# The last product pair of each output tile: 512 columns first, 256 columns second

## The chip, the cores and the metric

The kernel runs on one core of a Trainium2 chip. The metric is device time in microseconds, from runs that are timed without a profile; the kernel before has a median of 1256.36 us over 3 runs (1256.25 to 1256.43). Beside them there is one profiled execution with its trace.

## The reference

One layer of a streaming encoder over 256 positions and 2048 channels, in float32:

```python
h = _rmsnorm(x, norm_mix[i])
proj = h @ w_in[i]                                  # 2048 -> SSD and GLA inputs
mix = jnp.concatenate([y_ssd, y_gla], axis=-1) @ w_out[i]
x = x + mix
h = _rmsnorm(x, norm_ffn[i])
u = _causal_dwconv(h @ ffn_w_up[i], ffn_conv_w[i], ffn_conv_b[i])   # 2048 -> 11264
gate, val = jnp.split(u, [D_FF], axis=-1)
x = x + (jax.nn.silu(gate) * val) @ ffn_w_down[i]   # 5632 -> 2048
pg = jax.nn.sigmoid(_rmsnorm(x, norm_ple[i]) @ ple_w_gate[i])       # 2048 -> 2048
x = x + pg * (p[i] @ ple_w_proj[i])
return _rmsnorm(x, norm_final)
```

The change concerns the products from `w_out` on. The two mixers in front of them (a Mamba-2 scan and a gated linear attention) are left as they are.

## The kernel before

Everything is held with channels on the 128 partitions and the 256 positions along the free dimension. Weights stream from DRAM in chunks of 1 MB: a chunk (`raw`) holds 16 blocks of 128 x 128. ACT rounds each half chunk to float32r (`whi`, L185), and DVE takes the remainder (`wlo`, L186); the pool has 5 buffers of each, so two to three chunks are ready ahead of TensorE. Activations are split in the same way, into `act[:, 0, :]` (rounded) and `act[:, 1, :]` (remainder).

A block (m, k) of a weight contributes to output tile m in a PSUM bank of 512 columns. In the helper `mm2` one product has the rounded weights against both parts of the activation side by side, 512 columns wide (the hi product, L219); a second has the remainder of the weights against the rounded activation, 256 columns wide, into the lower half of the bank (the lo product, L220). For the last block of an output tile (`last`) the two stand the other way round: lo at L220, then hi at L222 with the stop flag. `mm3`, with three products of 256 columns, serves the input projection and the very last tile of the gate.

`project` walks a sequence of (m, k): the blocks of the first two tiles are interleaved, so that their last 4 or 5 k come after both; from the third tile on, a tile's blocks follow one another. A chunk is 16 blocks; with 16 blocks to a tile (output projection, up-projections, gate) a tile from the third on is one chunk, with 22 (down-projections) chunks begin in the middle of tiles. `project` is called six times: output projection (16 tiles of 16 blocks), up-projection (44 of 16) and down-projection (16 of 22) for the first half of the hidden width, the same for the second half, and the gate (16 of 16, the last through `mm3`).

When a tile's last product is issued, `evac` takes it: after the output and the down-projections DVE adds both halves of the bank to x (L917); after the up-projections and the gate ACT copies the upper half (L232) and DVE adds the lower (L233). Output tiles rotate over four banks (`pm_t`). TensorE's order is the program's order, written out by hand; ACT's, DVE's and the DMA queue's rows are ordered by a scheduler that works with dependences and an estimated timeline, in which the weight chunks have a raised priority. At the start of the first up-projection and of the gate, norms of the residual stream run between the products (`norm_task`), and the evictions that need the norm's result (`rb`, L331) follow it.

Of the kernel before, what the change touches and what calls it, by code (L numbers as in the profile page):

```python
# [15 lines left out]
T = 256  # L16
# [65 lines left out]


def steps(n_m, n_k, tail):
    """(m, k) in the order of the products: the last k of the first two m come after both."""
    cut = n_k - tail
    s = [(m, k) for m in (0, 1) for k in range(cut)]
    s += [(m, k) for m in (0, 1) for k in range(cut, n_k)]
    return s + [(m, k) for m in range(2, n_m) for k in range(n_k)]


SEQ16 = steps(16, KT, 4)
SEQ_UP = steps(2 * UPH, KT, 4)
SEQ_DN = steps(16, UPH, 5)


@with_exitstack
def trunk(ctx, tc, wst, wv, xin, pin, prm_d, cst_d, gku_d, out):
    nc = tc.nc
    V, S, G, PE = nc.vector, nc.scalar, nc.gpsimd, nc.tensor  # L100
# [12 lines left out]
    def slot(dtype=F32, shape=(128, 512)):  # L113
        return gpool.tile(list(shape), dtype, name="slot")
# [4 lines left out]
    def pmt():  # L119
        return pm.tile([128, 512], F32, name="pm_t")  # L120

    def pxt():
        return px.tile([128, 512], F32, name="px_t")
# [1 line left out]
    def v3(ap, n):  # L125
        return ap.rearrange("p (a b) -> p a b", a=n)

# [1 line left out]
    now = [0]  # L129
    tasks = []  # L130
    done = {}
# [1 line left out]
    def tick():  # L133
        now[0] += 1
        for t in list(tasks):
            if t[0] <= now[0]:
                d = next(t[1], None)
                if d == 0:
                    continue
                if d is None:  # L140
                    tasks.remove(t)
                else:
                    t[0] = now[0] + d
                break
# [8 lines left out]
        while any(done.get(k, 1 << 30) > now[0] for k in keys):  # L153
            yield 0

# [1 line left out]
    ready = {}  # L157

    def raw_tile():
# [45 lines left out]
    def chunk(c):  # L205
        load(c)
        load(c + 1)
        return ready.pop(c)

    def lhs(wt, j):  # L210
        hi, lo = wt[j // 8]
        w = slice((j % 8) * 128, (j % 8 + 1) * 128)
        return hi[:, w], lo[:, w]

    def mm2(ps, wt, j, act, first, last):
        hi, lo = lhs(wt, j)
        both = act.rearrange("p a t -> p (a t)")
        if not last:
            PE.matmul(ps, lhsT=hi, rhs=both, start=first, stop=False)  # L219
        PE.matmul(ps[:, 0:T], lhsT=lo, rhs=act[:, 0, :], start=False, stop=False)  # L220
        if last:
            PE.matmul(ps, lhsT=hi, rhs=both, start=False, stop=True)  # L222

    def mm3(ps, wt, j, act, first, last):
        hi, lo = lhs(wt, j)
        PE.matmul(ps, lhsT=hi, rhs=act[:, 0, :], start=first, stop=False)  # L226
        PE.matmul(ps, lhsT=hi, rhs=act[:, 1, :], start=False, stop=False)  # L227
        PE.matmul(ps, lhsT=lo, rhs=act[:, 0, :], start=False, stop=last)  # L228
# [5 lines left out]
        return t  # L234

    def project(base, seq, acts, n_k, evac, single=None):
        """Products of a weight stream in the order seq; evac(m, ps) when an output tile is whole."""
        ps = {}
        wt = None
        for n, (m, k) in enumerate(seq):  # L240
            if n % 16 == 0:
                wt = chunk(base + n // 16)
            if k == 0:
                ps[m] = pmt()
            if m == single:
                mm3(ps[m][:, 0:T], wt, n % 16, acts[k], k == 0, k == n_k - 1)
            else:
                mm2(ps[m], wt, n % 16, acts[k], k == 0, k == n_k - 1)
            if k == n_k - 1:
                evac(m, ps.pop(m))  # L250
            if n % TICK == TICK - 1:
                tick()

# [1 line left out]
    def pcol(i):  # L255
        return prm[:, i:i + 1]

# [73 lines left out]
        S.copy(out=keep, in_=ps)  # L331
        then(r, keep)

# [1 line left out]
    prm = const.tile([128, NPRM], F32, name="prm")  # L335
    x = const.tile([128, KT, T], F32, name="x")
    cst = const.tile([128, NCST], F32, name="cst")
# [33 lines left out]
    for m in range(KT):  # L371
        wt = ready[m // 8]
        if m % 2 == 0:
            ps = pmt() if m % 4 == 0 else pxt()
# [19 lines left out]
    for a in proj:  # L394
        store_proj(*a)

# [1 line left out]
    usuf_r = const.tile([128, 128], F32R, name="usuf_r")  # L398
    ones_r = const.tile([128, 128], F32R, name="ones_r")
    cbh = const.tile([128, 12], F32, name="cbh")  # L400
# [38 lines left out]
        S.activation(out=t, in_=c, func=AF.Tanh)  # L439
        V.scalar_tensor_tensor(out=out, in0=t, scalar=1.0, in1=c, op0=ALU.add, op1=ALU.mult)  # L440

# [1 line left out]
    gkl = const.tile([32, T], F32, name="gkl")  # L443
    G.memset(gkl, 1.0)
    dta = const.tile([128, 32], F32, name="dta")
# [73 lines left out]
        PE.matmul(ps[:, 16:32], lhsT=tri, rhs=a_tm[:, 16:32], start=True, stop=True)  # L519
        S.activation(out=esuf, in_=ps[:, 0:32], func=AF.Exp)  # L520

# [1 line left out]
    ssd_x = [None] * 8  # L523
    bT = slot()
    cT = slot()
# [194 lines left out]
                    mix[i] = split(y)  # L720
            yield from norm_task(ssd_sq[g], 512, then, 9)

# [1 line left out]
    gq = [slot(), slot()]  # L724
    gk = [slot(), slot()]
    gla = {}
# [119 lines left out]
        V.tensor_tensor(out=o, in0=o, in1=sg, op=ALU.mult)  # L846
        mix[8 + i] = split(o)

# [1 line left out]
    def ev_in(kind, i, ps):  # L850
        if kind == "conv":
            ev_conv(i, ps)
        elif kind == "q":
            ev_qk(gq, i, ps, 128.0 ** -0.5)
        elif kind == "k":
            ev_qk(gk, i, ps, 1.0)
            mark(("k", i))
        elif kind == "z":
            ev_z(i, ps)
        else:  # L860
            ev_g(i, ps)

    vps = None
    for ci, (kind, i) in enumerate(PLAN):
# [20 lines left out]
        if kind == "v":  # L885
# [3 lines left out]
            for kk in range(4):  # L889
                k = kc * 4 + kk  # L890
                hi, lo = wt[kk // 2]
# [11 lines left out]
        else:  # L903
            ps = pmt()
# [6 lines left out]
    while tasks:  # L911
        tick()

# [1 line left out]
    def add_res(i, ps):  # L915
        for h in range(2):
            V.tensor_tensor(out=x[:, i, :], in0=x[:, i, :], in1=ps[:, h * T:(h + 1) * T], op=ALU.add)  # L917
# [8 lines left out]
    sq_ffn = SumSq()  # L926
    xf = [None] * KT
    project(OFF_OUT, SEQ16, mix, KT, residual(sq_ffn, P_GFFN, xf))

# [1 line left out]
    state.clear()  # L931

    def delayed(f):
# [42 lines left out]
    for half in range(2):  # L976
        base = OFF_F0 if half == 0 else OFF_F1
        project(base, SEQ_UP, xf, KT, ev_up(half))
        if half == 0:
            project(base + N_UP, SEQ_DN, hid, UPH, add_res)  # L980
        else:
            sq_ple = SumSq()
            project(base + N_UP, SEQ_DN, hid, UPH, residual(sq_ple, P_GPLE, xg))

# [1 line left out]
    state.clear()  # L986
    sq_fin = SumSq()
    emb = {}
# [52 lines left out]
    start(first_emb())  # L1041
    project(OFF_GATE, SEQ16, xg, KT, delayed(ev_gate), single=KT - 1)

# [1 line left out]
    banks = {}  # L1045

    def turn(q, c):
# [126 lines left out]
```

## Time and profile before

| what | value |
|---|---|
| median of the timed runs | 1256.36 us (1256.25 to 1256.43) |
| profiled execution, first to last instruction (its span) | 1254.4 us |
| median less span | 1.96 us |
| TensorE products, busy | 1243.2 us (99%), 7707 products |
| TensorE weight loads, busy | 1110.7 us (89%) |
| DVE, ACT busy | 896.0 us (71%), 691.2 us (55%) |
| DMA share, mean HBM rate | 52.4%, 183 GB/s |
| mean granted TensorE clock | 0.999 |

The profiled execution has no time of its own other than its span; what lies around the span is taken as the difference to the median. Products overlap in the records: a 512-column product's row is some 398 ns long, yet the next one starts 0.24 us after it. What a product costs in a stream is therefore read from start to start and not from its length. The stages start at 313.25 (output projection), 403.68 (first up-projection), 652.88 (first down-projection), 777.23 (second up-projection), 1025.97 (second down-projection) and 1150.32 us (gate); the last tile's three-product blocks start at 1235.57.

### The profile page before, as it was taken

Reading aid. Unit: us, or ns where it says so; the run is one execution under the profiler, and the core shown is the slowest. Engines: PE = TensorE matmul, PEld = TensorE weight load, DVE = VectorE, ACT = ScalarE, POOL = GpSimd, SP = SyncE. Lnnn points to the kernel's source line nnn. Section 1 sums busy time; section 2 is a strip of 40 time slices with the busy share of each in tenths; the row PEclk is TensorE's granted clock in tenths of the full one; section 3 lists DMA queues with packets and bytes.
Section 4 is the critical chain, followed back from the end, with each engine's and each line's share of the span. In section 5 each row is a group of like instructions: output and inputs, shape, how many; then the busy total and the mean of one; then the engine's idle time right before and its main releaser. Section 6 shows DMA issues by size and latency. Waiting matters only on the chain.

```text
span 1254.4 us, 19554 instructions
## 1 busy us (share of the span) xinstructions
PE 1243.2 (99%) x7707; PEld 1110.7 (89%) x7707; DVE 896.0 (71%) x1531; ACT 691.2 (55%) x1144; POOL 2.9 (0%) x10
## 2 busy tenths in 40 slices
PE   9999999999999999999999999999999999999997
PEld 7999999999888888888888888888888888888886
DVE  7877665788777787777775555777777776666775
ACT  8685564565545565555553333555555554444664
POOL 0000000000000000000000000000000000000000
PEclk9999999999999999999999999999999999999999
DMA  9745353344555455555555555555555555556531
GB/s 332 295 156 172 124 202 135 137 167 168 198 174 199 168 202 173 196 179 191 187 183 193 178 197 174 198 173 197 183 186 191 179 196 193 199 172 223 197 131 67
DMA packets 36830, 231.01 MB, mean 184 GB/s; under 512 B 4209, under 2 KB 4593, under 8 KB 11138
## 3 DMA queue, kind: packets, MB, share of 16 engines
q1 hardware_dynamic: 36738, 229.76, 52.4%
q8 instruction: 60, 0.98, 0.3%
q14 instruction: 32, 0.26, 0.1%
HBM read 225.55 MB, written 4.19 MB: 183 GB/s over the span
## 4 chain that ended last, share of the span: by engine, by line
PE 97%; DVE 1%; ACT 1%; DMA 1%; SPq 0%; issue 0%; DVEq 0%
PE pm_t L219 46%; PE pm_t L220 25%; PE pm_t L226 6%; PE pm_t L228 6%; PE pm_t L227 6%; PE pm_t L222 3%; PE pm_t L897 1%; PE pm_t L898 1%; PE pm_t L896 1%; DMA raw<-in_wst_dram 1%; PE px_t L629 1%; DVE wlo L186 0%; PE px_t L792 0%; ACT xg L260 0%; PE px_t L288 0%; ACT whi L185 0%
## 5 line engine op out<-in xcount | busy, mean ns | idle before, releaser
L185 ACT CAST whi<-raw 128x1024 fp32r<-128x1024 f32 (+3 forms) x444 | 444.2, 1005 | 513.8 <-PE pm_t L219 244.1
L186 DVE TENSOR_TENSOR wlo<-raw,whi 128x1024 fp32r<-128x1024 f32 (+3 forms) x444 | 517.1, 1168 | 273.3 <-ACT whi L185 270.5
L219 PE MATMUL pm_t<-xg,whi 128*128 128x512 f32 x1545 | 549.8, 398 | 0.0
L220 PE MATMUL pm_t<-xg,wlo 128*128 128x256 f32 x1648 | 446.0, 281 | 0.0
L219 PEld LDWEIGHTS pm_t<-xg,whi 128*128 128x128 f32 x1545 | 290.3, 188 | 66.5
L219 PE MATMUL pm_t<-slot,whi 128*128 128x512 f32 x912 | 324.1, 398 | 0.0
L220 PEld LDWEIGHTS pm_t<-xg,wlo 128*128 128x128 f32 x1648 | 311.1, 189 | 10.1
L220 PE MATMUL pm_t<-slot,wlo 128*128 128x256 f32 x960 | 261.8, 281 | 0.0
L219 PEld LDWEIGHTS pm_t<-slot,whi 128*128 128x128 f32 x912 | 171.4, 188 | 40.2
L220 PEld LDWEIGHTS pm_t<-slot,wlo 128*128 128x128 f32 x960 | 181.3, 189 | 4.7
L226 PE MATMUL pm_t<-xg,whi 128*128 128x256 f32 x592 | 170.1, 287 | 0.0
L228 PE MATMUL pm_t<-xg,wlo 128*128 128x256 f32 x592 | 167.4, 283 | 0.0
L227 PE MATMUL pm_t<-xg,whi 128*128 128x256 f32 x592 | 167.4, 283 | 0.0
L226 PEld LDWEIGHTS pm_t<-xg,whi 128*128 128x128 f32 x592 | 113.0, 191 | 1.2 <-issue 1.0
L227 PEld LDWEIGHTS pm_t<-xg,whi 128*128 128x128 f32 x592 | 113.0, 191 | 0.5 <-issue 0.2
L228 PEld LDWEIGHTS pm_t<-xg,wlo 128*128 128x128 f32 x592 | 113.0, 191 | 0.0
L962 DVE SCALAR_TENSOR_TENSOR tmp<-tmp,prm 128x255 f32<-128x255 f32 (+1 forms) x176 | 84.5, 480 | 3.9 <-ACT tmp L959 1.0
L917 DVE TENSOR_TENSOR x<-x,pm_t 128x256 f32<-128x256 f32 x96 | 40.1, 419 | 25.7 <-PE pm_t L222 24.4
L959 ACT ACTIVATE tmp<-tmp,prm 128x256 f32<-128x256 f32 x88 | 52.4, 596 | 0.4 <-DVE tmp L957 0.4
L233 DVE TENSOR_TENSOR tmp<-pm_t,tmp 128x256 f32<-128x256 f32 x103 | 43.0, 418 | 0.7 <-ACT tmp L232 0.7
L222 PE MATMUL pm_t<-xg,whi 128*128 128x512 f32 x103 | 41.2, 400 | 0.0
L232 ACT COPY tmp<-pm_t 128x256 f32<-128x256 f32 x103 | 37.5, 364 | 1.4 <-PE pm_t L222 1.4
(210 smaller groups left out, 836.0 us busy)
## 6 DMA issues: line engine op xcount, KB each, us to landing
raw<-in_wst_dram SPq DMA_DIRECT2D x200, 1024.0 KB, 4.9
raw<-in_wv_dram SPq DMA_DIRECT2D x8, 704.0 KB, 4.1
raw<-in_wv_dram SPq DMA_DIRECT2D x8, 352.0 KB, 8.3
x<-in_xin_dram SPq DMA_DIRECT2D x4, 512.0 KB, 8.4
pp<-slot SPq DMA_DIRECT2D x8, 256.0 KB, 8.2
slot<-pp SPq DMA_DIRECT2D x8, 256.0 KB, 5.5
out_dram<-raw SPq DMA_DIRECT2D x8, 256.0 KB, 3.2
raw<-in_wst_dram SPq DMA_DIRECT2D x2, 512.0 KB, 7.4
```

The lines of the kernel that those rows point to most:

```text
L185: S.copy(out=hi[:, sl], in_=raw[:, rs])
L186: V.tensor_tensor(out=lo[:, sl], in0=raw[:, rs], in1=hi[:, sl].bitcast(F32), op=ALU.subtract)
L219: PE.matmul(ps, lhsT=hi, rhs=both, start=first, stop=False)
L220: PE.matmul(ps[:, 0:T], lhsT=lo, rhs=act[:, 0, :], start=False, stop=False)
L222: PE.matmul(ps, lhsT=hi, rhs=both, start=False, stop=True)
L226: PE.matmul(ps, lhsT=hi, rhs=act[:, 0, :], start=first, stop=False)
L227: PE.matmul(ps, lhsT=hi, rhs=act[:, 1, :], start=False, stop=False)
L228: PE.matmul(ps, lhsT=lo, rhs=act[:, 0, :], start=False, stop=last)
L233: V.tensor_tensor(out=t, in0=ps[:, 0:T], in1=t, op=ALU.add)
L917: V.tensor_tensor(out=x[:, i, :], in0=x[:, i, :], in1=ps[:, h * T:(h + 1) * T], op=ALU.add)
L959: S.activation(out=c, in_=v, func=AF.Identity, scale=pcol(P_FW + 176 + ch), bias=pcol(P_FB + ch))
L962: V.scalar_tensor_tensor(out=c[:, s:], in0=v[:, :T - s], scalar=pcol(P_FW + 88 * (2 - s) + ch), in1=c[:, s:], op0=ALU.mult, op1=ALU.add)
```

## The change

`mm2` no longer asks whether the block is the last of its tile: the hi product of 512 columns always comes first, the lo product of 256 columns second, and the stop flag goes from the hi to the lo product. The number of products, their operands and the weight loads stay. (Comment lines and a docstring are emptied, and the functions behind move up by three lines.)

```diff
     def mm2(ps, wt, j, act, first, last):
         hi, lo = lhs(wt, j)
         both = act.rearrange("p a t -> p (a t)")
-        if not last:
-            PE.matmul(ps, lhsT=hi, rhs=both, start=first, stop=False)
-        PE.matmul(ps[:, 0:T], lhsT=lo, rhs=act[:, 0, :], start=False, stop=False)
-        if last:
-            PE.matmul(ps, lhsT=hi, rhs=both, start=False, stop=True)
+        PE.matmul(ps, lhsT=hi, rhs=both, start=first, stop=False)
+        PE.matmul(ps[:, 0:T], lhsT=lo, rhs=act[:, 0, :], start=False, stop=last)
```

TensorE, first up-projection, the border between two output tiles (pm_t_5153 and pm_t_5208), before; whi and wlo are the weight halves, xg the split activations:

```order
2976 L219 MATMUL pm_t_5153<-xg_4788,whi_5097 128x512
2977 L220 MATMUL pm_t_5153<-xg_4788,wlo_5098 128x256
2978 L220 MATMUL pm_t_5153<-xg_4839,wlo_5098 128x256
2979 L222 MATMUL pm_t_5153<-xg_4839,whi_5097 128x512
2980 L219 MATMUL pm_t_5208<-xg_4111,whi_5145 128x512 [waits DVE_49,PE_49]
2981 L220 MATMUL pm_t_5208<-xg_4111,wlo_5146 128x256
```

The same place in the change (L218 and L219 are now the two products):

```order
2976 L218 MATMUL pm_t_5153<-xg_4788,whi_5097 128x512
2977 L219 MATMUL pm_t_5153<-xg_4788,wlo_5098 128x256
2978 L218 MATMUL pm_t_5153<-xg_4839,whi_5097 128x512
2979 L219 MATMUL pm_t_5153<-xg_4839,wlo_5098 128x256
2980 L218 MATMUL pm_t_5208<-xg_4111,whi_5145 128x512 [waits DVE_49,Activation_49]
2981 L219 MATMUL pm_t_5208<-xg_4111,wlo_5146 128x256 [waits DVE_49]
```

Rows 2978 and 2979 have changed places; the next tile's first product, with its wait, now stands behind a product of 256 columns.

TensorE in the first down-projection, before, where a weight chunk (whi_7323) begins in the middle of a tile:

```order
4306 L219 MATMUL pm_t_7355<-slot_6158,whi_7319 128x512
4307 L220 MATMUL pm_t_7355<-slot_6158,wlo_7320 128x256
4308 L219 MATMUL pm_t_7355<-slot_6265,whi_7323 128x512 [waits Activation_49]
4309 L220 MATMUL pm_t_7355<-slot_6265,wlo_7324 128x256 [waits DVE_49]
4310 L219 MATMUL pm_t_7355<-slot_6372,whi_7323 128x512
```

Here a hi product with a wait stands behind a lo product in the kernel before too; nothing moves here.

ACT at the start of the first up-projection, before (rb is the norm's result, L185 casts weights, L959 and L966 are the convolution's bias and the Silu, L232 the eviction's copy):

```order
329 L331 COPY rb<-px_t 128x256
330 L185 CAST whi<-raw 128x1024
331 L959 ACTIVATE tmp<-tmp,prm 128x256
332 L232 COPY tmp<-pm_t 128x256
333 L185 CAST whi<-raw 128x1024
334 L966 ACT_TABLE_LOAD
335 L966 ACTIVATE tmp<-tmp 128x256
336 L959 ACTIVATE tmp<-tmp,prm 128x256
337 L232 COPY tmp<-pm_t 128x256
338 L185 CAST whi<-raw 128x1024
```

The same stretch in the change (L328 is the copy of rb, L956, L963 and L229 the others):

```order
329 L328 COPY rb<-px_t 128x256
330 L956 ACTIVATE tmp<-tmp,prm 128x256
331 L229 COPY tmp<-pm_t 128x256
332 L185 CAST whi<-raw 128x1024
333 L963 ACT_TABLE_LOAD
334 L963 ACTIVATE tmp<-tmp 128x256
335 L956 ACTIVATE tmp<-tmp,prm 128x256
336 L229 COPY tmp<-pm_t 128x256
337 L185 CAST whi<-raw 128x1024 x2
```

The first cast goes behind L956 and L229, the second behind the table load, the Silu and the next tile's two rows; the third follows it at once. Some rows move likewise on ACT at the gate's start, and DVE's subtractions with them; the rest of ACT and DVE, POOL and the DMA queue are in the same order.

## Rows read from the trace of the kernel before

**Rows 1.** The page's busy table and sliced clock: busy us (share) and count

```profile
span 1254.4 us, 19554 instructions
...
PE 1243.2 (99%) x7707; PEld 1110.7 (89%) x7707; DVE 896.0 (71%) x1531; ACT 691.2 (55%) x1144; POOL 2.9 (0%) x10
...
PEclk9999999999999999999999999999999999999999
```

**Rows 2.** The chain that ended last, shares by line

```profile
PE pm_t L219 46%; PE pm_t L220 25%; PE pm_t L226 6%; PE pm_t L228 6%; PE pm_t L227 6%; PE pm_t L222 3%; PE pm_t L897 1%; PE pm_t L898 1%; PE pm_t L896 1%; DMA raw<-in_wst_dram 1%; PE px_t L629 1%; DVE wlo L186 0%; PE px_t L792 0%; ACT xg L260 0%; PE px_t L288 0%; ACT whi L185 0%
```

**Rows 3.** Costliest groups: line, count, busy us and mean ns, idle before

```profile
L219 PE MATMUL pm_t<-xg,whi 128*128 128x512 f32 x1545 | 549.8, 398 | 0.0
...
L222 PE MATMUL pm_t<-xg,whi 128*128 128x512 f32 x103 | 41.2, 400 | 0.0
```

**Rows 4.** Timeline of TensorE, one up-projection tile: start us, length us

```profile
562.43 0.40 PE L219 MATMUL pm_t<-xg,whi 128*128 128x512 f32 x1
562.66 0.28 PE L220 MATMUL pm_t<-xg,wlo 128*128 128x256 f32 x1
562.77 0.40 PE L219 MATMUL pm_t<-xg,whi 128*128 128x512 f32 x1
...
567.37 0.40 PE L219 MATMUL pm_t<-xg,whi 128*128 128x512 f32 x1
567.61 0.40 PE L220 MATMUL pm_t<-xg,wlo 128*128 128x256 f32 x2
567.85 0.40 PE L222 MATMUL pm_t<-xg,whi 128*128 128x512 f32 x1
568.08 0.40 PE L219 MATMUL pm_t<-xg,whi 128*128 128x512 f32 x1
```

**Rows 5.** Line L219's instructions: count, ns min/median/max, first and last start

```profile
L219 PE MATMUL pm_t<-xg,whi x1545: 387/398/476, 403.7 to 1234.9; 128*128 128x512 f32 x194
...
L219 PE MATMUL pm_t<-slot,whi x912: 387/398/403, 313.3 to 1149.6; 128*128 128x512 f32 x183
```

**Rows 6.** Timeline of TensorE, the gate's last tile through mm3

```profile
1235.57 0.28 PE L226 MATMUL pm_t<-xg,whi 128*128 128x256 f32 x1
...
1239.52 0.28 PE L226 MATMUL pm_t<-xg,whi 128*128 128x256 f32 x1
```

**Rows 7.** Timeline of TensorE, first products of the last three stages

```profile
777.23 0.40 PE L219 MATMUL pm_t<-xg,whi 128*128 128x512 f32 x1
...
1025.97 0.40 PE L219 MATMUL pm_t<-slot,whi 128*128 128x512 f32 x1
...
1150.32 0.40 PE L219 MATMUL pm_t<-xg,whi 128*128 128x512 f32 x1
```

**Rows 8.** Timeline, a chunk's start inside a down-projection tile

```profile
669.69 0.28 PE L220 MATMUL pm_t<-slot,wlo 128*128 128x256 f32 x1
669.70 0.19 PEld L219 LDWEIGHTS pm_t<-slot,whi 128*128 128x128 f32 x1
669.81 0.40 PE L219 MATMUL pm_t<-slot,whi 128*128 128x512 f32 x1
```

**Rows 9.** Who waited for whom: us in total, times, longest

```profile
ACT whi L185 <- PE pm_t L219: 244.1, 189, 1.8
```

**Rows 10.** Timeline of ACT, start of the first up-projection

```profile
425.12 0.60 ACT L959 ACTIVATE tmp<-tmp,prm 128x256 f32<-128x256 f32 x1
...
430.52 1.05 ACT L185 CAST whi<-raw 128x1024 fp32r<-128x1024 f32 x1
```

**Rows 11.** Timeline, same stretch: an eviction's sum, a wlo, two tiles' first products

```profile
426.79 0.42 DVE L233 TENSOR_TENSOR tmp<-pm_t,tmp 128x256 f32<-128x256 f32 x1
...
432.50 0.40 PE L219 MATMUL pm_t<-xg,whi 128*128 128x512 f32 x1
...
435.13 1.22 DVE L186 TENSOR_TENSOR wlo<-raw,whi 128x1024 fp32r<-128x1024 f32 x1
...
443.71 0.40 PE L219 MATMUL pm_t<-xg,whi 128*128 128x512 f32 x1
```

## The prediction

> **What bounds the kernel now.** I began with the busy table and the sliced clock: TensorE is busy for 1243.2 of 1254.4 us, and its granted clock is at 9 (90% or more) in all 40 slices, the upper of its two levels, 2.4 GHz [rows 1]. Since the page says that a busy TensorE is modelled, I went on to the chain of waits and to the costliest groups. The lines of the changed helper hold most of the chain that ended last: L219 46%, L220 25%, L222 3% [rows 2]. The groups end with the idle time in front of them: 0.0 us at L219 and at L222 [rows 3]. So from the output projection on, products follow one another without a gap, ACT and DVE wait for TensorE and not the reverse, and the time is the sum of the intervals from the start of one product to the start of the next. What the change is worth has to be read from these intervals.
>
> **How an interval is read.** The timeline prints starts to 10 ns. In the middle of an output tile a hi product starts (rounded weights, 512 columns), 0.23 or 0.24 us later the lo product (their remainder, 256 columns), and 0.11 or 0.12 us after that the next hi one: 562.43, 562.66, 562.77 [rows 4]. From 562.43 to the fifteenth hi product at 567.37 there are 14 such pairs: 4.94 / 14 = 352.9 ns for a pair [rows 4]. Averaged over all starts of the stage (first and last in [rows 5]) hi to lo is 236.1 ns (2457 of them) and lo to next hi 116.8 ns (2304).
>
> **The change part by part.** It touches the end of each output tile alone. There are 151 such ends: 16 + 44 + 16 + 44 + 16 + 15 by the loops (the last tile of the gate goes through mm3); 103 of them, 44 + 44 + 15, are the L222 row that reads xg [rows 3].
>
> *Removed:* before, an end reads lo, lo', hi', and then the next tile's hi (the prime marks the tile's last weight block). Its three intervals, averaged in the same way over the 151 ends, are 119.6 (lo to lo'), 119.9 (lo' to hi') and 235.7 ns (hi' to next hi): 475.2 ns together. One of them is in [rows 4]: the L220 pair at 567.61, hi' at 567.85, the next tile at 568.08, which is 0.47 from 567.61.
>
> *Added:* now it reads lo, hi', lo', next hi: 116.8 + 236.1 + 116.8 = 469.7 ns. Same instructions, same weight loads, same columns; only the neighbours differ. A 256-column product costs some 3 ns more when the other product next to it is also of 256 columns. The three-product tile at the end is a second witness: from 1235.57 to 1239.52 there are 33 products of 256 columns in a row, 3.95 / 33 = 119.7 ns each [rows 6]. The hi products cost the same in both orders.
>
> *The sum:* 475.2 - 469.7 = 5.5 ns at an end, times 151 = 0.83 us. A check that needs no averaging: the second up-projection has 704 weight blocks and 44 ends and runs from 777.23 to 1025.97, 248.74 us; the down-projection behind it has 352 and 16 and runs from there to 1150.32, 124.35 us, twice which is 248.70 [rows 7]. The same 704 blocks with 12 more ends take 0.04 us more, 3 ns an end by starts good to 0.01 us, so anything from 2 to 6. It gives 0.3 to 0.9 us for 151. I take 5.5, since it rests on all ends and not on one difference of large numbers.
>
> *What the trace of before does not show* is a new tile's first hi product (another PSUM bank, start flag, a wait for its weights) right behind a 256-column product of the old tile. Bounds by the nearest rows: among the starts averaged above, the cheapest single intervals that stand for the three are 113, 224 and 113 ns (450 together, 25 below 475.2), the dearest 124, 241 (nine in ten lie below it; two of 315 follow the norm's one-column products) and 124 (489, 14 above). Times 151 that is -3.8 to +2.1 us, as if every end hit an extreme. The nearest row is a weight chunk that begins in the middle of a down-projection tile: there a hi product carrying a wait for its weights already stands behind a lo product, 669.69 to 669.81, 0.12 us [rows 8]; 40 such average 117.2 ns, 0.4 above the others. So I value it at 117.
>
> *Buffers and evictions.* The last use of a whi buffer comes 116.8 ns earlier or so and that of a wlo later by about as much against the tile's end; ACT, which waits 244.1 us for L219 before its casts [rows 9], starts them accordingly, and DVE's subtractions come behind the casts. Evictions: the tile is whole some 5 ns sooner, since what goes into it is the same and the stream is that much shorter. ACT's copy of columns 256 to 511 no longer needs the tile's last product and could begin some 0.12 us sooner; TensorE never waits for evictions, so it is worth nothing.
>
> *Reordered rows on ACT and DVE.* At the start of the first up-projection and of the gate the casts of later weights move behind evictions on ACT, with DVE's subtractions after them. What moves in front of a cast there (two L959, two copies, the table load and the Silu) all stands between 425.12 and 430.52 before, so a cast comes less than 5.4 us later [rows 10]. The cover is the lead of the weights: in the tightest place DVE ends a wlo at 435.13 + 1.22 = 436.35, and the chunk's first hi product starts at 443.71, so 7.4 us ahead [rows 11]. The banks have 5.3 us: tile 1's sum ends at 426.79 + 0.42 = 427.21 and the product that needs the bank again starts at 432.50 [rows 11]; in the changed row that tile's copy stands earlier, not later. So the moves cost nothing; with the cover gone, each us beyond it would be a us.
>
> **From the span to the time.** The sum is made against a span of 1254.4 us; the median of the runs is 1256.36, so 1.96 us lie around the span, and the change does not touch them. 1256.36 - 0.83 = 1255.53: I predict 1255.5 us.
>
> **Rivals.**
>
> *Columns alone decide (no change, 1256.4).* If an interval depended only on the columns of the product that opens it, lo-lo-hi-hi and lo-hi-lo-hi would cost the same, and the 3 ns would be a matter of where the records put a start. For it: the differences are below the timeline's step. Against it: 151 ends, the run of 33, and the stage lengths agree in sign. The Trainium skill, "TensorE: Matmul & The Clock Gate", Back-to-back issue gap, gives the warm gap of an isolated product as N/2.4 + 2.5 ns, a function of columns alone, which would make the change worth 0; the rows here are longer than its figures (236 and 117 to 120) and do depend on the neighbour.
>
> *The new tile's weights are exposed (slower, 1264 to 1267).* Before, the load for a new tile's first product ran beside a 512-column product of 0.23 us; now it has a 256-column one of 0.117, and a load's record is 0.19 us long [rows 8]. If the wait held the load back until that product started and the load had to end first, an end would cost 190 - 117 = 73 ns more: 8.6 us for the 118 ends at which a weight chunk begins too, 11.0 us for all 151, less 0.8. Against it: inside a tile each hi load already runs beside a 256-column product, and the same wait in the same place costs 0.4 ns on average [rows 8]. It decides from the point at which weights are cast late, and they lead by over 7 us. The Trainium skill's page "TensorE: Matmul & The Clock Gate", What overlaps and what doesn't, says that a weight load overlaps products in flight only when its row group differs, which speaks for this rival; here every load covers all 128 rows and starts with the product before it (669.70 beside 669.69 [rows 8]), so the trace does not agree.
>
> *The moved casts stall TensorE (slower).* It needs over 7.4 us of delay where less than 5.4 can arise; a stall of 3 us at one of the two places would give 1258.5.
>
> *More than 0.2% faster.* 2.5 us over 151 ends is 17 ns each, close to the cheapest single intervals every time. Nothing in the averages speaks for it.
>
> **How the numbers follow.** My forecast, an end 3 to 6 ns cheaper (1255.4 to 1255.9), 0.80; columns alone, 0.11; exposed weights, 0.03; stalled casts, 0.03; much faster, 0.03. About 0.2%, or 2.5 us, is what a measurement of this kernel can tell from no change. The first two cases lie within it, 0.91; faster 0.04 with a little of the forecast's tail; slower 0.05, since a short stall stays within it. The range leaves out the last three and takes in no change, with part of the bounds of the unseen border on both sides, 5 ns an end or 0.8 us: 1254.7 to 1257.2.
>
> **What would show it.** The profile after should have 2608 hi and 2608 lo products in strict alternation, no pair of L220 rows merged as x2 at a tile's end, and a new tile's first product 0.11 to 0.12 us behind the last lo; the second up-projection 44 x 5.5 ns = 0.24 us shorter (248.50) and a down-projection 16 x 5.5 = 0.09 us (124.26); no wait of TensorE at the helper's lines. The prediction is wrong if that first product comes at 0.18 us or later, if TensorE waits at the up-projection's or the gate's start, or if the stage lengths do not shrink at all.

## The result, and the profile after

The changed kernel takes 1241.80 us (median of 4 runs, 1240.75 to 1241.90) against 1256.35 for the kernel before: ratio 0.9881, 95% interval [0.9867, 0.9895]. It is 14.5 us faster; 0.8 us were forecast.

The page after, lines that answer to [rows 1] and [rows 3]; in the groups the columns are count, busy us, mean ns and idle before:

```profile
span 1240.0 us, 19470 instructions
...
PE 1228.7 (99%) x7707; PEld 1103.7 (89%) x7707; DVE 896.3 (72%) x1531; ACT 692.1 (56%) x1144; POOL 3.0 (0%) x10
...
PEclk9999999999999999999999999999999999999999
...
L218 PE MATMUL pm_t<-xg,whi 128*128 128x512 f32 x1648 | 572.0, 394 | 0.0
```

As many products as before, the same clock, no idle time in front of them; TensorE's busy time itself is 14.5 us shorter. The mean record of a hi product (rounded weights, 512 columns) went from 398 to 394 ns, which points to the whole stream and not to the borders alone. Where the time went, the first products of the stages and of the gate's last tile tell (start us, length us):

```profile
313.86 0.40 PE L218 MATMUL pm_t<-slot,whi 128*128 128x512 f32 x1
...
404.31 0.40 PE L218 MATMUL pm_t<-xg,whi 128*128 128x512 f32 x1
...
649.23 0.40 PE L218 MATMUL pm_t<-slot,whi 128*128 128x512 f32 x1
...
771.25 0.40 PE L218 MATMUL pm_t<-xg,whi 128*128 128x512 f32 x1
...
1015.30 0.40 PE L218 MATMUL pm_t<-slot,whi 128*128 128x512 f32 x1
...
1137.33 0.40 PE L218 MATMUL pm_t<-xg,whi 128*128 128x512 f32 x1
...
1221.21 0.28 PE L223 MATMUL pm_t<-xg,whi 128*128 128x256 f32 x1
```

| stage | tile ends changed | before us | after us | gained us |
|---|---|---|---|---|
| output projection | 16 | 90.43 | 90.45 | -0.02 |
| first up-projection | 44 | 249.20 | 244.92 | 4.28 |
| first down-projection | 16 | 124.35 | 122.02 | 2.33 |
| second up-projection | 44 | 248.74 | 244.05 | 4.69 |
| second down-projection | 16 | 124.35 | 122.03 | 2.32 |
| gate, to its last tile | 15 | 85.25 | 83.88 | 1.37 |

Together 14.97 us; the output projection started 0.61 us later in this execution, which leaves the 14.4 us between the spans. The first row is the odd one: 16 ends were changed in the same way as elsewhere, and nothing came of it. The starts of tiles in the kernel after say how the stages differ, one tile of 16 blocks in the output projection and one in the first up-projection:

```profile
370.39 0.40 PE L218 MATMUL pm_t<-slot,whi 128*128 128x512 f32 x1
...
376.04 0.40 PE L218 MATMUL pm_t<-slot,whi 128*128 128x512 f32 x1
...
471.73 0.40 PE L218 MATMUL pm_t<-xg,whi 128*128 128x512 f32 x1
...
477.17 0.27 PE L219 MATMUL pm_t<-xg,wlo 128*128 128x256 f32 x1
477.28 0.40 PE L218 MATMUL pm_t<-xg,whi 128*128 128x512 f32 x1
```

5.65 us a tile in the first, 5.55 in the second, with the same products in the same order. A block is one hi and one lo product (the remainder of the weights, 256 columns). From hi product to hi product, with the lo products in between left out, a stretch of each kind:

```profile
406.07 0.40 PE L218 MATMUL pm_t<-xg,whi 128*128 128x512 f32 x1
...
406.43 0.40 PE L218 MATMUL pm_t<-xg,whi 128*128 128x512 f32 x1
...
406.78 0.40 PE L218 MATMUL pm_t<-xg,whi 128*128 128x512 f32 x1
...
407.13 0.40 PE L218 MATMUL pm_t<-xg,whi 128*128 128x512 f32 x1
...
440.19 0.39 PE L218 MATMUL pm_t<-xg,whi 128*128 128x512 f32 x1
...
440.53 0.40 PE L218 MATMUL pm_t<-xg,whi 128*128 128x512 f32 x1
...
440.88 0.39 PE L218 MATMUL pm_t<-xg,whi 128*128 128x512 f32 x1
```

To the nanosecond of the trace, blocks (hi start to hi start) repeat as 361, 349, 350 in the first stretch, which is 353.3 on average, and as 350, 343 or 344 in the second, 346.7. I call the first the slow pattern and the second the two-block fast pattern. Both go on unchanged over hundreds of blocks, past chunk and tile borders. A third, the one-block fast pattern, has 345 to 348 every time. In the kernel before nearly all blocks away from tile ends follow the slow one. The changed kernel goes over to the two-block fast one here, at the norm's four one-column products (L285), and stays there to the end of the stage and through all later ones:

```profile
413.85 0.40 PE L218 MATMUL pm_t<-xg,whi 128*128 128x512 f32 x1
414.08 0.28 PE L219 MATMUL pm_t<-xg,wlo 128*128 128x256 f32 x1
414.20 0.50 PE L285 MATMUL px_t<-cst,acc 128*128 128x1 f32 x4
414.56 0.48 PE L218 MATMUL pm_t<-xg,whi 128*128 128x512 f32 x1
414.88 0.28 PE L219 MATMUL pm_t<-xg,wlo 128*128 128x256 f32 x1
414.99 0.40 PE L218 MATMUL pm_t<-xg,whi 128*128 128x512 f32 x1
...
415.34 0.39 PE L218 MATMUL pm_t<-xg,whi 128*128 128x512 f32 x1
```

From there 2324 blocks follow, and at 6.6 ns less each they make 15.3 us; the measured 14.97 is less because four tiles of the kernel before, two in the first up-projection and two in the gate, were in a fast pattern already (below).

### The profile page after: what moved, and what is told of

It is laid out like the page before. It is cut to its first block, busy times and chain, and to the rows that moved or that the text cites. A ratio compares the mean times of both kernels' runs of the same rounds, so it can differ in the third digit from the quotient of the medians.

```text
span 1240.0 us, 19470 instructions
## 1 busy us (share of the span) xinstructions
PE 1228.7 (99%) x7707; PEld 1103.7 (89%) x7707; DVE 896.3 (72%) x1531; ACT 692.1 (56%) x1144; POOL 3.0 (0%) x10
## 4 chain that ended last, share of the span: by engine, by line
PE 96%; ACT 1%; DVE 1%; DMA 1%; SPq 0%; issue 0%; DVEq 0%
PE pm_t L218 49%; PE pm_t L219 24%; PE pm_t L223 6%; PE pm_t L225 6%; PE pm_t L224 6%; PE pm_t L894 1%; PE pm_t L895 1%; PE pm_t L893 1%; DMA raw<-in_wst_dram 1%; PE px_t L626 1%; ACT xg L257 0%; ACT whi L185 0%; PE px_t L789 0%; ACT tmp L278 0%; PE px_t L285 0%; SPq L165 0%
## 5 line engine op out<-in xcount | busy, mean ns | idle before, releaser
L185 ACT CAST whi<-raw 128x1024 fp32r<-128x1024 f32 (+3 forms) x444 | 443.4, 1004 | 498.5 <-PE pm_t L218 391.3
L218 PE MATMUL pm_t<-xg,whi 128*128 128x512 f32 x1648 | 572.0, 394 | 0.0
L219 PE MATMUL pm_t<-xg,wlo 128*128 128x256 f32 x1648 | 456.6, 277 | 0.0
L218 PEld LDWEIGHTS pm_t<-xg,whi 128*128 128x128 f32 x1648 | 309.0, 188 | 71.6
L218 PE MATMUL pm_t<-slot,whi 128*128 128x512 f32 x960 | 334.6, 395 | 0.0
L219 PEld LDWEIGHTS pm_t<-xg,wlo 128*128 128x128 f32 x1648 | 309.4, 188 | 0.0
L219 PE MATMUL pm_t<-slot,wlo 128*128 128x256 f32 x960 | 266.9, 278 | 0.0
L218 PEld LDWEIGHTS pm_t<-slot,whi 128*128 128x128 f32 x960 | 180.1, 188 | 42.5
L219 PEld LDWEIGHTS pm_t<-slot,wlo 128*128 128x128 f32 x960 | 180.5, 188 | 0.0
L225 PE MATMUL pm_t<-xg,wlo 128*128 128x256 f32 x592 | 167.4, 283 | 0.0
L223 PEld LDWEIGHTS pm_t<-xg,whi 128*128 128x128 f32 x592 | 113.0, 191 | 1.2 <-issue 1.0
L224 PEld LDWEIGHTS pm_t<-xg,whi 128*128 128x128 f32 x592 | 113.0, 191 | 0.4 <-issue 0.2
L959 DVE SCALAR_TENSOR_TENSOR tmp<-tmp,prm 128x255 f32<-128x255 f32 (+1 forms) x176 | 84.7, 481 | 4.5 <-ACT tmp L956 1.5
L956 ACT ACTIVATE tmp<-tmp,prm 128x256 f32<-128x256 f32 x88 | 52.7, 598 | 1.1 <-DVE tmp L954 1.0
L229 ACT COPY tmp<-pm_t 128x256 f32<-128x256 f32 x103 | 37.4, 364 | 1.3 <-PE pm_t L219 1.3
L954 DVE TENSOR_TENSOR tmp<-tmp,rb 128x256 f32<-128x256 f32 x88 | 37.1, 421 | 1.4
```

Source lines behind the costliest of these rows:

```text
L185: S.copy(out=hi[:, sl], in_=raw[:, rs])
L229: S.copy(out=t, in_=ps[:, T:2 * T])
L956: S.activation(out=c, in_=v, func=AF.Identity, scale=pcol(P_FW + 176 + ch), bias=pcol(P_FB + ch))
L959: V.scalar_tensor_tensor(out=c[:, s:], in0=v[:, :T - s], scalar=pcol(P_FW + 88 * (2 - s) + ch), in1=c[:, s:], op0=ALU.mult, op1=ALU.add)
```

## The experiments

**The theory, and two rivals.** Cycles: the stream of hi and lo products settles into one of these patterns and stays in it until something breaks the alternation, a swapped pair or products of another kind; what comes out depends on the pattern and on the block of it that is hit. In the kernel before, each tile end is such a break, and nearly each restarts the slow pattern. Border cost: each of the 151 ends cost 96 ns by itself. Other engines: the earlier release of weight buffers or the other order of ACT and DVE made TensorE's reads faster.

**One pair swapped back.** On the changed kernel, in `project` (and in `mm2` the argument `lo_first`, which issues lo before hi):

```diff
-                mm2(ps[m], wt, n % 16, acts[k], k == 0, k == n_k - 1)
+                mm2(ps[m], wt, n % 16, acts[k], k == 0, k == n_k - 1,
+                    lo_first=base == OFF_F0 and (m, k) == (10, 15))
```

> The changed kernel with one single pair put back: in the first up-projection, the last block of output tile 10 has its lo product before its hi product; everything else stays hi first. Theory of the cycles (the stream of hi and lo products has a slow self-repeating pattern of 353.3 ns a block and fast ones of 346.7 ns, and only a disturbance changes from one to the other): the swap is a disturbance, and if it lands in the slow pattern, that stays for all 1964 blocks up to the gate's norm, +6.6 ns each, +13.0 us, 1254.8 us; if it lands in a fast one, 1241.8 us, nothing between. Rival, each border costs by itself (14.5 us / 151 ends = 96 ns): +0.1 us, 1241.9 us. Rival, other engines (earlier release of weight buffers, other order of ACT and DVE): 1241.8 us.

1242.64 us, ratio to before 0.9890 [0.9875, 0.9904]. The timeline at the swap (L219 is hi, L220 lo, L222 the swapped hi):

```profile
465.14 0.40 PE L219 MATMUL pm_t<-xg,whi 128*128 128x512 f32 x1
465.37 0.40 PE L220 MATMUL pm_t<-xg,wlo 128*128 128x256 f32 x2
465.61 0.39 PE L222 MATMUL pm_t<-xg,whi 128*128 128x512 f32 x1
465.84 0.40 PE L219 MATMUL pm_t<-xg,whi 128*128 128x512 f32 x1
```

The swap did change the pattern, from the two-block to the one-block fast one, for all of the 1964 blocks up to the gate's norm. These two cost the same, so nothing is lost there (first up-projection 244.93 us). The gate's norm products then met the one-block pattern and left the slow one behind: from its first to its last hi product the gate takes 84.93 us against 83.54 in the changed kernel. That loss, some 680 us after the swap and 1.4 us in size, was in no expectation; a border cost does not give it, but by the time alone the rivals were not yet excluded.

**The same one block earlier** (`(10, 14)`):

> As the run before, but the swapped pair is one block earlier, the last but one of tile 10, so that it meets the fast two-block pattern at its other block and lies inside a tile, not at a border. Theory of the cycles: again all or nothing, 1254.8 us or 1241.8 us, and perhaps the other one of the two than for the last block. Rival, border cost: not a border, 1241.8 to 1241.9 us. Rival, other engines: 1241.8 us.

1242.59 us, 0.9890 [0.9875, 0.9905]; again one-block fast from the swap on, slow in the gate (84.94). The other block of the two-block pattern made no difference.

**The change in one half of the FFN only.** The condition is `k == n_k - 1 and base not in (OFF_F0, OFF_F0 + N_UP)` for the first half, with OFF_F1 for the second; 60 ends changed in each.

> The change in the first up- and down-projection alone (60 of the 151 tile ends); the other 91 ends as before, lo first at the last block. Theory of the cycles: slow in the output projection, fast from the norm in the first up-projection to the end of the first down-projection (4.3 + 2.3 us gained), slow again from the first swapped end of the second up-projection: 1256.35 - 6.6 = 1249.7 us. Rival, border cost at 96 ns an end: 60 x 0.096 = 5.8 us, 1250.6 us. Rival, other engines: no number.

> The change in the second up- and down-projection alone, again 60 of the 151 tile ends. Theory of the cycles: no disturbance comes at these ends any more, but the stream arrives in the slow pattern from the first half's last end and nothing takes it out, so nothing is gained: 1256.3 us, and both stages as long as before (248.7 and 124.3 us). Rival, border cost at 96 ns an end: 5.8 us, 1250.6 us.

First half: 1249.45 us, 0.9945 [0.9930, 0.9960]. Second half: 1256.24 us, 0.9998 [0.9988, 1.0007]. Stage starts of the first kernel from the second up-projection on:

```profile
770.64 0.40 PE L219 MATMUL pm_t<-xg,whi 128*128 128x512 f32 x1
...
1019.19 0.40 PE L219 MATMUL pm_t<-slot,whi 128*128 128x512 f32 x1
...
1143.54 0.40 PE L219 MATMUL pm_t<-xg,whi 128*128 128x512 f32 x1
```

and of the second kernel:

```profile
777.26 0.40 PE L219 MATMUL pm_t<-xg,whi 128*128 128x512 f32 x1
...
1025.99 0.40 PE L219 MATMUL pm_t<-slot,whi 128*128 128x512 f32 x1
...
1150.38 0.40 PE L219 MATMUL pm_t<-xg,whi 128*128 128x512 f32 x1
```

In the second kernel these two stages have no swapped end any more and still take 248.73 and 124.39 us, as in [rows 7]: they arrive slow and nothing takes them out. The same 60 changed ends are worth 7.1 us in one place and nothing in the other. This ends the border cost as an explanation.

**The norm's products four blocks earlier, and four later.** No pair is touched, only where the four one-column products and what depends on them stand:

```diff
         def gen():
-            yield 6
+            yield 5
```

> The changed kernel with the norm's one-column products (and all that follows from them) four blocks earlier in the first up-projection and in the gate. Theory of the cycles: these products are the disturbance that takes the stream from the slow to the fast pattern in the changed kernel, and what comes out depends on the block of the slow three-block pattern on which they fall; four blocks shift that by one. So either it still ends fast, 1241.8 us, or the stream stays slow for the 2025 blocks to the gate's norm, +13.4 us, 1255.2 us. Rival, border cost, and rival, other engines: 1241.8 us, as no tile border and no buffer changes.

> As the run before, but four blocks later, the third of the three places in the slow pattern. Theory of the cycles: 1241.8 us (a few blocks' 6.6 ns more) or 1255.2 us; at least one of the three places should end slow, since disturbances in the kernel before did. Rival, border cost, and rival, other engines: 1241.8 us.

Earlier: 1256.97 us, 1.0006 [0.9997, 1.0016]: the whole gain of the change is gone. Later (`yield 7`): 1243.92 us, 0.9903 [0.9888, 0.9918]; its first up-projection goes over to the one-block fast pattern (244.96 us), and the gate's norm throws it back (84.91 us). The earlier one:

```profile
403.59 0.40 PE L218 MATMUL pm_t<-xg,whi 128*128 128x512 f32 x1
...
412.07 0.50 PE L285 MATMUL px_t<-cst,acc 128*128 128x1 f32 x4
...
653.01 0.40 PE L218 MATMUL pm_t<-slot,whi 128*128 128x512 f32 x1
...
777.39 0.40 PE L218 MATMUL pm_t<-xg,whi 128*128 128x512 f32 x1
...
1026.13 0.40 PE L218 MATMUL pm_t<-slot,whi 128*128 128x512 f32 x1
```

249.42 us for the up- and 124.38 for the down-projection, with strict alternation at all 151 ends: the slow pattern needs no swapped end to go on. In its second up-projection TensorE and ACT have the same instructions in the same order as in the changed kernel (DVE too, but for one row that crosses the stage's end), and TensorE waits for nothing; it takes 248.74 us there and 244.05 in the changed kernel. The same stretch of program has two lengths, by what came some 360 us before it. It is not chance from one execution to the next: the ten of this kernel lie between 1256.42 and 1257.72 us, the four of the changed one between 1240.75 and 1241.90. With three places in the slow pattern the three outcomes were slow, two-block fast and one-block fast.

**No weight stream.** The stream of weights ends early in the output projection, and all later products read the last chunk that was loaded, so the kernel leaves out the rest of the weights:

```diff
-        if c not in ready and c < N_CHUNK:
+        if c > OFF_OUT + 3:
+            ready[c] = kept[0]
+        elif c not in ready and c < N_CHUNK:
```

> The changed kernel without the weight stream from the fifth chunk of the output projection on: no transfers, casts or remainders of weights, all later products read the weights of that chunk. Theory of the cycles, if they are TensorE's own: the slow pattern in the output projection and the fast one after the norm with the same 353.3 and 346.7 ns a block, 1241.8 us (or 1255 us if the norm's products meet the slow pattern at another block). Rival, other engines (contention of ACT, DVE or transfers with TensorE's reads, or waits for them): the products get faster without them, or the patterns go away; at the 320 ns that 768 columns take at 2.4 GHz the 2608 blocks would be 70 us shorter, and any such gain speaks for it.

1242.22 us, 0.9889 [0.9875, 0.9904]. Busy table and stage starts (L222 is hi here):

```profile
PE 1228.8 (99%) x7707; PEld 1103.7 (89%) x7707; DVE 536.0 (43%) x1211; ACT 387.8 (31%) x824; POOL 3.0 (0%) x10
```

```profile
404.27 0.40 PE L222 MATMUL pm_t<-xg,whi 128*128 128x512 f32 x1
...
649.19 0.40 PE L222 MATMUL pm_t<-slot,whi 128*128 128x512 f32 x1
...
771.22 0.40 PE L222 MATMUL pm_t<-xg,whi 128*128 128x512 f32 x1
```

ACT has 304 us less to do and DVE 360; the stages are as long to 0.01 us (244.92 and 122.03), slow in the output projection and fast after the norm at the same block. Weight traffic and the release of weight buffers have no part in the patterns. Evictions still ran, but not all the time. In two stretches of this run nothing but TensorE works (columns: stretch and its us; busy us and count of PE, PEld, DVE, ACT, POOL; granted clock; DMA share and GB/s):

```profile
406.76:414.10 7.34, 7.34 (x44) 6.36 (x43) 0.00 (x0) 0.00 (x0) 0.00 (x0) 1.00 0.00 0
653.72:662.90 9.18, 9.18 (x55) 8.05 (x54) 0.00 (x0) 0.00 (x0) 0.00 (x0) 1.00 0.00 0
```

The first, before the norm's products, repeats 361, 349, 350 ns from block to block throughout, the second 350, 343 or 344. So no contention with another engine or a transfer keeps either pattern up.

**Two swaps, and one in the output projection**, each a forecast from changes of pattern already seen. The conditions are `(m, k) in ((10, 15), (20, 15))` in the first up-projection, and `base == OFF_OUT and n == 6`:

> The changed kernel with two pairs put back in the first up-projection, the last blocks of output tiles 10 and 20. The first alone turned the two-block fast pattern into the one-block one and cost nothing there. Theory of the cycles: in the kernel before, a swapped tile end that met the one-block pattern (third tile of the first up-projection) went over to the slow one, so the second swap should do the same here: slow from its next block, 1796 blocks to the end of the second down-projection and the gate's first 28, +6.6 ns each, 11.9 us, so 1253.7 us. Rival, border cost: two ends, +0.2 us, 1242.0 us. Rival, other engines: 1241.8 us.

> The changed kernel with one pair swapped (lo first) at the seventh block of the output projection, on the place of the slow pattern at which two swapped ends of the kernel before led to the one-block fast pattern. Theory of the cycles: the output projection is fast from there, -1.9 us, but the norm's products then meet the one-block pattern, which ended slow in the gate of the one-swap run; so slow from the norm in the first up-projection, +13.4 us: 1253.3 us in all. If the norm's products leave it fast, 1239.9 us. Rival, border cost, and rival, other engines: 1241.8 to 1241.9 us.

Two swaps: 1253.57 us, 0.9976 [0.9966, 0.9986], where 1253.7 was expected. A tile after the first and one after the second swap:

```profile
471.71 0.39 PE L219 MATMUL pm_t<-xg,whi 128*128 128x512 f32 x1
...
477.26 0.39 PE L219 MATMUL pm_t<-xg,whi 128*128 128x512 f32 x1
...
527.28 0.40 PE L219 MATMUL pm_t<-xg,whi 128*128 128x512 f32 x1
...
532.93 0.40 PE L219 MATMUL pm_t<-xg,whi 128*128 128x512 f32 x1
```

5.55, then 5.65 us. One swapped pair of 2608 cost nothing up to the gate and 1.4 us there; a second one cost 11 us (1253.57 against 1242.64). In the output projection: 1254.87 us, 0.9987 [0.9977, 0.9996], against 1253.3; the projection did get fast (88.79 us), the norm's products did throw the stream back, and the gate too stayed slow (85.13 us from first to last hi product, 83.54 in the changed kernel), which I had not counted (1.6 us).

**Extra products to leave the slow pattern early.** Behind the eighth block of the output projection, and in a second kernel behind the fifth (`n == 4`):

```diff
+            if base == OFF_OUT and n == 7:
+                kick = pxt()
+                for c in range(2):
+                    PE.matmul(kick[:, c:c + 1], lhsT=ident, rhs=ones[:, 0:1], start=True, stop=True)
             if k == n_k - 1:
                 evac(m, ps.pop(m))
```

> The changed kernel with two extra one-column float32 products (four in the records) behind the eighth block of the output projection, on the same place of the slow pattern as the norm's products have in the first up-projection; their result is not used. Theory of the cycles: the output projection turns fast there: 276 blocks to the norm's products at 6.6 ns, -1.8 us, plus some 0.35 us for the products, 1240.3 us, if the norm's products, now met in a fast pattern, do not throw the stream back into the slow one (then some 1254 us). Rival, border cost, and rival, other engines: +0.35 us, 1242.1 us.

> The changed kernel with the two extra one-column float32 products behind the fifth block of the output projection instead of the eighth: three blocks earlier, so the same place of the three-block slow pattern. Theory of the cycles: fast from the sixth block on and through the norm, the output projection 1.2 us shorter than in the changed kernel as behind the eighth block (89.2 us), 1.4 us in all, 1240.4 us beside 1241.8 us. If the place in the pattern did not matter or were not stable from execution to execution, the output projection could as well stay slow: +0.4 us, 1242.2 us.

> The changed kernel itself, timed beside the next run on one chip, to see whether extra products in the output projection gain more than a measurement can miss. All theories: 1241.8 us.

Eighth block: 1239.87 us, 0.9875 [0.9858, 0.9891]. Fifth block: 1239.55 us (1239.21 to 1240.61), 0.9868 [0.9852, 0.9885], beside the changed kernel on the same chip at 1241.68 us (1240.95 to 1242.13), 0.9884 [0.9869, 0.9898]. The fifth block's timeline:

```profile
313.27 0.40 PE L218 MATMUL pm_t<-slot,whi 128*128 128x512 f32 x1
...
315.03 0.50 PE L249 MATMUL px_t<-cst 128*128 128x1 f32 x4
...
402.49 0.40 PE L218 MATMUL pm_t<-xg,whi 128*128 128x512 f32 x1
```

The output projection takes 89.22 us instead of 90.45 and the first up-projection 244.73 instead of 244.92, 1.4 us in all, as expected; the other 0.7 us between the medians most likely lie in front of it, where the stage's start moved between 312.8 and 314.2 us from run to run. All executions of this kernel were faster than all of the changed one. It leaves nothing of the computation out and beats both kernels. The intervals of the two ratios overlap, so the 1.4 us over the changed kernel rest on the stage lengths. The changed kernel's second trace has every stage as long as the first one's, to 0.01 us.

## Why the prediction was wrong

What bounds the kernel was right: TensorE's stream, with no wait, and its time is the sum of the starts' intervals. That casts, evictions and buffers have slack was right too; the kernel without the weight stream is as long. The order of products after the change is the one forecast, and a new tile's first product comes 0.11 to 0.12 us behind the old tile's last one (477.17 to 477.28 above). The stage lengths were not: the second up-projection became 4.69 us shorter and not 0.24, a down-projection 2.33 and not 0.09.

The step that failed is the pricing in "How an interval is read" and "The sum": one average for each kind of interval, 236.1 and 116.8 ns, taken as a price that a product has with its neighbours and would keep after the change. These averages mix a slow pattern with a few fast tiles. A block costs 353.3 or 346.7 ns with the same neighbours, and which one is decided by the last break in the alternation, hundreds of blocks back. So the term "5.5 ns at an end, times 151" priced the wrong thing twice. At the ends themselves there was nothing to gain: 16 changed ends in the output projection gave -0.02 us, and a slow tile of 16 blocks takes 5.65 us with a swapped end [rows 4] and without one (370.39 to 376.04), so what an end costs in the averages, the blocks beside it give back. And the 2457 blocks away from the ends, left out by "it touches the end of each output tile alone", carried nearly the whole gain. The check by stage lengths could not see it, since both stages in it were slow; it compared the slow pattern with itself.

The trace of before held the sign. The sixth tile of the first up-projection starts at 432.50 [rows 11], and the next one here:

```profile
438.06 0.39 PE L219 MATMUL pm_t<-xg,whi 128*128 128x512 f32 x1
```

5.56 us, swapped end included, where the next one takes 5.65 (to 443.71 [rows 11]), as in [rows 4]. One tile that differs from the rest by 1.6% without a wait was the sign that the stream has a second state. A bound with all blocks in it, 0.09 us less for 16 blocks and so 5.6 ns for each of 2608, would have been 14.7 us; the bounds of the prediction, -3.8 to +2.1 us, were drawn at the ends alone. The rival "More than 0.2% faster" had the right direction, but looked for 17 ns at an end, which no end gave.

Of the rivals, columns alone is refuted: the same columns cost two prices. By the gap that the Trainium skill, "TensorE: Matmul & The Clock Gate", Back-to-back issue gap, gives for an isolated product, a function of columns alone, the time would have stayed unchanged. In this stream the measurement decides against it: 353.3 or 346.7 ns a block. Exposed weights and stalled casts did not occur.

## What to carry to other kernels

When TensorE streams without waits, look at the starts of products to the nanosecond over whole tiles and ask whether the pattern is one or several; a mean over all of them hides it. If a stage has tiles of two lengths with equal work, anything that breaks the regular order may be a switch, whose effect is worked out from the blocks behind it and not from its own length. Place such breaks (norm products, odd ends) by trial, and profile after each move: four one-column products moved by four blocks were worth 15 us here.

## What the runs showed of the hardware that was not expected

A strict alternation of 512- and 256-column products with a weight load each has at least three self-sustaining timings at the granted clock of 2.4 GHz (0.998 of it in the changed kernel): 361, 349, 350 ns a block, 350 and 343 or 344, and 345 to 348. What was seen to change them (columns: the pattern that the break met; cells: the pattern behind it):

| what breaks the stream | slow | two-block fast | one-block fast |
|---|---|---|---|
| a swapped pair | slow at nearly all ends of before; one-block fast in the output projection run | one-block fast (two runs) | slow (two swaps) |
| the norm's four products | slow, two-block or one-block fast by the block hit | two-block fast (gate after) | slow (gate, one swap) |

They outlast borders of tiles, chunks and stages, and neither the weight transfers nor ACT's and DVE's weight work have a part in them; they also go on where no other engine and no transfer is busy. What in TensorE sets them, and why a break leads to the one or the other, no run here shows.
